# Attention with the keys on the partitions instead of transposed probabilities

## The chip, the cores and the metric

The kernel runs on one core of one Trainium2 chip. A core has a matrix engine (TensorE, in the profile PE, with its weight loads shown apart as PEld), a vector engine (DVE), a scalar engine (ACT), a general engine (POOL), DMA queues, a working memory of 128 partitions (SBUF) and an accumulator memory of eight banks (PSUM). A matmul loads a *stationary* operand (the weights, at most 128 x 128) and streams a *moving* operand of up to 512 columns past it; both have the contracted index on the partitions, and the result has the stationary operand's columns on its partitions. The metric is device time in microseconds (us); less is better. The kernel before has three timed runs and one profiled one.

## The reference

One inference step of a two-layer trunk for 512 latent tokens ("sample") and 128 context tokens ("prompt"), model width 1024. Layer 0 is gated grouped-query attention, layer 1 a bidirectional gated linear recurrence; each has an adaptive modulation of its input, an output projection and a layer norm. Everything is float32. Only the attention of layer 0 matters here:

```python
def _block_attention(q, k, v):          # q: 16 heads of 64; k, v: 4 heads of 64
    ...
    s = jnp.einsum('bqkgd,bskd->bkgqs', q_blk.astype(jnp.float32), kf) * scale
    p = jax.nn.softmax(s, axis=-1)
    return jnp.einsum('bkgqs,bskd->bqkgd', p, vf).astype(q.dtype)
```

A sample query attends to 640 keys (128 cached and 512 of its own); a prompt query attends to the 128 prompt keys. The result is multiplied by SiLU of a gate (tile `gs`) before the output projection.

## The kernel before, in words

**Number format of the scores.** Queries and keys are split into a high part and a low part, each of which the PE takes in one pass (type fp32r). For a key head `c`, tile `Xs[c]` holds four query heads with their 64 high rows and 64 low rows on the two halves of the 128 partitions (which half is which depends on `c`). `kk` holds the high part of the keys twice, once in each half; `klo` holds the low part of the keys in the half of the high queries and zeros in the other half. So one product with `kk` gives (high q + low q) times high k, and one with `klo` adds high q times low k (`score_mms`, lines 923 and 924). The probabilities and the values are plain float32, which the PE takes in several passes; the profile shows each such matmul as two records with a weight load each, and a transpose as one.

**Units of work.** The 32 sample units are (key head `c` of 4) x (query head `h` of 4) x (half `qh` of the 512 queries, so 256 queries). After four of the eight sample units of each `c` comes one prompt unit. A sample unit has these parts in `sample_unit`:

- `front(i)`, for the two blocks of 128 queries: four matmuls of 320 columns make the scores with the queries on the partitions and the 640 keys along the row (L923, L924, tile `sc`, a pair of PSUM banks); DVE takes the row's maximum, negated (L1018, `nm`); ACT takes the exponential of 640 columns with that as its bias and gives the row's sum too (L1023, `p`, `su`); two steps later DVE takes the reciprocal (L1028) and POOL scales the row (L1029).
- `trans`: ten PE transposes of 128 x 128 bring the probabilities to keys on partitions (L1036, tile `pt`), and ACT or DVE copies them to SBUF (L928, `pts`).
- `pair`/`apply`, once for two heads: ten matmuls (L950, `av_mms`) with 64 columns of the values as weights and 256 probabilities moving; the two heads lie on the two halves of the output's partitions, so that the result (`pot`) is already turned as the output projection needs it. DVE multiplies it into the gate (L955, `av_out`).

**Order of the work.** `att_gen` yields after each such part. While the attention of head `c` runs, the query projection of head `c+1` (`q_gen`: L389 to L391, norm, rotary positions, split, transposes L734), the modulation of the second layer (L312) and the loads of the next weights run as side work: `weave` advances it after each yield by a number of steps from a written table, `SIDE_AT`. `side.until("q1")` and so on force the projection to be complete before the first scores that need it. The whole first half of the program, attention included, is one block in which a planner may reorder the instructions of an engine by a simulated timeline; a few are pinned to the order of the program. The first fronts are issued in the lead-in, among the last gate projections (`gps`, L380 to L382); their exponentials are held back until that is done.

**PSUM during attention.** Two pairs of banks for scores (`b2`), three single banks (`b1`: transposes, query projections, modulation) and one (`pop`) for the result: eight in all.

## Time and profile before

| what | value |
| --- | --- |
| median of three runs | 819.64 us (819.39 to 822.28) |
| profiled execution: its time / its span | 820.92 us / 819.2 us |
| PE busy, PEld busy | 792.4 us, 700.9 us |
| DVE, ACT, POOL busy | 598.3, 447.0, 215.1 us |
| granted PE clock, mean | 0.993 |
| stretch with attention on PE | from 130.7 us (first score) to 324.5 us (last product with the values) |

How to read it: the span is the time from the first to the last profiled instruction; the execution's own time lies 1.7 us above it. "Busy" of PE is the union of records whose ends are modelled, and matmuls overlap, so the rate of the PE is read from the distance between the *starts* of successive records, not from their mean length. In a timeline row such as `229.94 1.03 PE L1036 MATMUL ... x8` the first number is the start in us, the second the length of the merged piece, x8 the number of records in it.

### The profile page before, as it was taken

Reading aid. Unit: us, or ns where it says so; the run is one execution under the profiler, and the core shown is the slowest. Engines: PE = TensorE matmul, PEld = TensorE weight load, DVE = VectorE, ACT = ScalarE, POOL = GpSimd, SP = SyncE. Lnnn points to the kernel's source line nnn. Section 1 sums busy time; section 2 is a strip of 40 time slices with the busy share of each in tenths; the row PEclk is TensorE's granted clock in tenths of the full one; section 3 lists DMA queues with packets and bytes.
Section 4 is the critical chain, followed back from the end, with each engine's and each line's share of the span. In section 5 each row is a group of like instructions: output and inputs, shape, how many; then the busy total and the mean of one; then the engine's idle time right before and its main releaser. Section 6 shows DMA issues by size and latency. Waiting matters only on the chain.

```text
span 819.2 us, 19274 instructions
## 1 busy us (share of the span) xinstructions
PE 792.4 (97%) x7953; PEld 700.9 (86%) x7953; DVE 598.3 (73%) x1083; ACT 447.0 (55%) x890; POOL 215.1 (26%) x261
## 2 busy tenths in 40 slices
PE   8999999999999989999999999999999999999994
PEld 6789999878888766888899999998999999897874
DVE  4567767686678885676799787868787876788376
ACT  2252545566566786132565666757484855766242
POOL 0124001353434843011500224122240404131121
PEclk9999999999999999999999999999999999999998
DMA  9944344234130150621431342324242344232341
GB/s 327 395 158 157 104 155 134 100 110 150 52 129 28 36 197 18 240 103 50 141 104 54 100 118 76 104 69 125 64 134 72 103 102 162 70 110 74 136 153 77
DMA packets 36630, 98.12 MB, mean 120 GB/s; under 512 B 5296, under 2 KB 12480, under 8 KB 36544
## 3 DMA queue, kind: packets, MB, share of 16 engines
q1 hardware_dynamic: 25872, 78.95, 28.7%
q0 software_dynamic: 4768, 14.18, 5.8%
q10 hardware_dynamic: 5904, 3.78, 1.6%
q8 instruction: 62, 1.02, 0.5%
q14 instruction: 24, 0.20, 0.1%
HBM read 86.06 MB, written 10.83 MB: 118 GB/s over the span
## 4 chain that ended last, share of the span: by engine, by line
PE 80%; DVE 8%; DMA 4%; ACT 3%; issue 2%; POOL 2%; SPq 0%; DVEq 0%; ACTq 0%; POOLq 0%
PE vgps L1383 8%; PE vgps L1379 4%; PE outp L1213 4%; PE outp L1215 4%; PE outp L1214 4%; PE rps L1451 4%; PE pot L950 3%; PE rps L1405 3%; PE rps L1407 3%; PE rps L1406 3%; PE pt L1036 3%; PE rps L1453 3%; PE rps L1452 3%; PE acc L568 3%; PE lv L1682 2%
## 5 line engine op out<-in xcount | busy, mean ns | idle before, releaser
L1029 POOL TENSOR_SCALAR p<-p,rc 128x640 f32<-128x640 f32 x64 | 56.9, 894 | 115.5 <-DVE rc L1028 98.3
L1720 POOL COPY At<-near 32x160 f32<-32x160 f32 x32 | 15.0, 469 | 191.8 <-PE lv L1688 173.7
L1023 ACT ACTIVATE p<-sc,nm 128x640 f32<-128x640 f32 x64 | 51.1, 801 | 25.2 <-DVE nm L1018 15.5
L1018 DVE TENSOR_REDUCE nm<-sc 128x1 f32<-128x640 f32 x64 | 51.7, 816 | 12.7 <-PE sc L924 12.6
L1405 PE MATMUL rps<-h1hi,rw 128*128 128x320 f32 x176 | 55.4, 315 | 0.0
L1407 PE MATMUL rps<-h1hi,rw 128*128 128x320 f32 x176 | 54.5, 310 | 0.1
L1406 PE MATMUL rps<-h1lo,rw 128*128 128x320 f32 x176 | 54.5, 309 | 0.0
L1036 PE MATMUL pt<-small,p 128*128 128x128 f32 x320 | 49.0, 277 | 3.0 <-DVE pts L928 1.2
L1383 PE MATMUL vgps<-rw,h1hi 128*128 128x512 f32 x180 | 48.3, 392 | 0.0
L1655 ACT COPY kc<-A 128x640 f32<-128x640 f32 x47 | 37.5, 798 | 18.5 <-DVE A L1706 12.5
L1036 PEld LDWEIGHTS pt<-small,p 128*128 128x128 f32 x320 | 36.5, 140 | 12.0 <-issue 5.6
L928 ACT COPY pts<-pt 128x512 f32<-128x512 f32 x64 | 36.1, 589 | 14.8 <-PE pt L1036 14.6
L923 PE MATMUL sc<-kk,X 128*128 128x320 f32 x128 | 42.4, 340 | 1.8 <-ACT p L1023 1.6
L1726 ACT COPY At<-lv 32x160 f32<-32x160 f32 (+1 forms) x48 | 15.8, 329 | 49.6 <-PE lv L1688 49.2
L950 PE MATMUL pot<-pts,vv 128*64 128x256 f32 x320 | 38.3, 384 | 2.1 <-DVE pts L928 2.0
L380 PE MATMUL gps<-hhi,whi 128*128 128x320 f32 x128 | 40.0, 312 | 0.1
L381 PE MATMUL gps<-hlo,whi 128*128 128x320 f32 x128 | 39.6, 309 | 0.0
L382 PE MATMUL gps<-hhi,wlo 128*128 128x320 f32 x128 | 39.5, 309 | 0.0
L1383 PEld LDWEIGHTS vgps<-rw,h1hi 128*128 128x128 f32 x180 | 33.1, 188 | 6.6
L924 PE MATMUL sc<-klo,X 128*128 128x320 f32 x128 | 38.6, 310 | 0.0
L1383 PE MATMUL vgps<-wspare,h1hi 128*128 128x512 f32 x140 | 38.1, 394 | 0.0
L389 PE MATMUL qmm<-whi,hhi 128*128 128x256 f32 x120 | 35.0, 292 | 0.1
(347 smaller groups left out, 2623.2 us busy)
## 6 DMA issues: line engine op xcount, KB each, us to landing
raw<-in_rec_w_in SPq DMA_DIRECT2D x40, 512.0 KB, 3.8
raw<-in_ada_m SPq DMA_DIRECT2D x16, 512.0 KB, 8.3
raw<-in_attn_w_in SPq DMA_DIRECT2D x16, 512.0 KB, 4.6
raw<-in_ada_s SPq DMA_DIRECT2D x16, 512.0 KB, 3.7
adaraw<-in_ada_c SPq DMA_DIRECT2D x11, 512.0 KB, 5.4
raw<-in_attn_w_out SPq DMA_DIRECT2D x8, 512.0 KB, 4.1
raw<-in_rec_w_out SPq DMA_DIRECT2D x8, 512.0 KB, 3.6
raw<-in_ada_c SPq DMA_DIRECT2D x5, 512.0 KB, 4.4
```

Source lines behind the costliest of these rows:

```text
L380: nc.tensor.matmul(ps[:, :320], w.hi(k)[:, c], hhi[:, k, t], start=(k == 0), stop=False)
L381: nc.tensor.matmul(ps[:, :320], w.hi(k)[:, c], hlo[:, k, t], start=False, stop=False)
L923: nc.tensor.matmul(out, X[:, h, t0:t0 + P], kk[:, c, k0:k1], start=True, stop=False)
L950: nc.tensor.matmul(pot[j * HD:(j + 1) * HD, :CW], vv[:, slot, c * HD:(c + 1) * HD], moving[j], start=first, stop=last)
L1018: nc.vector.tensor_reduce(nm[:, 0:1], sc[:, :, :320], AX.XY, ALU.max, negate=True)
L1023: return nc.scalar.activation(halves(p[:]), sc[:, :, :320], AF.Exp, bias=nm[:, 0:1], accum_out=su[:, 0:1])
L1029: nc.gpsimd.tensor_scalar(p, p, rs[:, 0:1], 1.0, ALU.mult, ALU.mult)
L1036: nc.tensor.transpose(pt[:, i * 256 + q * P:i * 256 + (q + 1) * P], ps[q][:, (k0 + i) * P:(k0 + i + 1) * P], ident)
L1383: nc.tensor.matmul(out, h1hi[:, k, t], wvg[i][:, k % 4].rearrange("p e n -> p (e n)"), start=(k == 0), stop=(k == KT - 1))
L1405: nc.tensor.matmul(ps[:, j, :320], hi[:, k, :], h1hi[:, k, t], start=(k == 0), stop=False)
L1406: nc.tensor.matmul(ps[:, j, :320], hi[:, k, :], h1lo[:, k, t], start=False, stop=False)
L1407: nc.tensor.matmul(ps[:, j, :320], lo[:, k, :], h1hi[:, k, t], start=False, stop=(k == KT - 1))
```

## The change

The scores are made a second time with the keys on the partitions, so that the probabilities come out of the exponential already as the product with the values needs them, and nothing of them is transposed.

- `top(i)` makes the scores as before, but with the high keys alone (two matmuls of 320 columns in place of four), only to take the row's maximum `nm`.
- `row()` makes a copy `x2` of the unit's 256 queries (ACT), turns the two columns of negated maxima into a row by two float32 matmuls (weights: the column repeated 128 times; moving: the identity) and copies that row into one partition `r` of the low half of `x2` (ACT).
- In `klo` that partition, until now zero, is set to one for the 640 sample keys. So the product of `klo` with `x2` adds the low keys' part and minus the maximum at once.
- `probs(k0, m)`, for blocks of 128 keys: one matmul with `kk` and one with `klo` as weights, 256 queries moving, into a bank of a new pool `st`; ACT takes the exponential of up to 512 columns, with neither bias nor sum.
- `apply()`, now for each unit: the probabilities (128 keys x 128 queries) are the weights, and 65 columns move: the 64 values of the key head and a column of ones (`vv` has 65 columns a head), whose product is the sum of the row. Ten matmuls a unit. After the second head of a pair, DVE takes four reciprocals and scales 256 columns (`ob`); two steps later (`D_TURN`) two transposes turn them (`turn`) and `av_out` multiplies them into the gate as before.
- POOL no longer scales anything in a sample unit. The held exponentials of the lead-in are gone.
- PSUM: one pair of banks for `top` instead of two, two single banks `st`; `b1` (three) and `pop` (one) stay. `bank_any` goes round seven places.
- `weave` takes rates by key head (`SIDE_RATES`) instead of the table. A unit now yields seven times: probs, top, apply of the unit before, probs, row of the next unit, top, probs.
- The loads and stores of the values (`cache_v`, `new_v`) move pieces of 64 numbers, because a row of `vv` is no longer contiguous.

```diff
-SIDE_AT = (
-    ...
+D_TURN = 2
+SIDE_RATES = (0.66, 0.55, 0.62, 0.15)
-def weave(main, side, steps):
-    for n, _ in enumerate(main):
-        for _ in range(int(steps[n]) if n < len(steps) else 1):
+def weave(main, side, phase, rates):
+    credit = 0.0
+    for _ in main:
+        credit += rates[phase()]
+        while credit >= 1.0:
+            credit -= 1.0
             side.step()
...
+    for e in range(2):
+        nc.gpsimd.memset(klo[HD * (1 - e):HD * (1 - e) + 1, e::2, :NT].bitcast(F32), 1.0)
-    vv = kvp.tile([P, 6, CW], F32, name="vv")
+    vv = kvp.tile([P, 6, NKV, HD + 1], F32, name="vv")
+    nc.gpsimd.memset(vv[:, :, :, HD:], 1.0)
...
-        pools["b2"] = ph.st.enter_context(pool("b2", 2, space=PSUM))
+        pools["b2"] = ph.st.enter_context(pool("b2", 1, space=PSUM))
+        pools["st"] = ph.st.enter_context(pool("st", 2, space=PSUM))
...
-        def front(i):
+        def top(i):
             sc = bank2("sc")
             for n, (k0, k1) in enumerate(HALVES):
-                score_mms(sc[:, n, :320], Xs[c], c, h, (2 * qh + i) * P, k0, k1)
+                nc.tensor.matmul(sc[:, n, :320], Xs[c][:, h, q0 + i * P:q0 + (i + 1) * P], kk[:, c, k0:k1], start=True, stop=True)
             nc.vector.tensor_reduce(nm[:, 0:1], sc[:, :, :320], AX.XY, ALU.max, negate=True)
...
-        def trans(k0, m):
...
-        def pair():
...
+        def row():
+            x2 = u["x2"] = sm.tile([P, CW], F32R, tag="x2", name="x2", bufs=2)
+            nc.scalar.copy(x2, Xs[c][:, h, q0:q0 + CW].bitcast(F32))
+            ps = bank1("row")
+            for i in range(2):
+                nc.tensor.matmul(ps[:, i * P:(i + 1) * P], view(u["nm", i], 0, [[0, P]]), ident, start=True, stop=True)
+            nc.scalar.copy(x2[r:r + 1, :], ps[r:r + 1, :CW])
+        def probs(k0, m):
+            if k0 == 0:
+                u["p"] = sm.tile([P, TT, CW], F32, tag="p", name="p", bufs=4)
+            ps = pools["st"].tile([P, 512], F32, tag="st", name="st")
+            for i in range(m):
+                k, out = slice((k0 + i) * P, (k0 + i + 1) * P), ps[:, i * CW:(i + 1) * CW]
+                nc.tensor.matmul(out, kk[:, c, k], Xs[c][:, h, q0:q0 + CW], start=True, stop=False)
+                nc.tensor.matmul(out, klo[:, c, k], u["x2"], start=False, stop=True)
+            last_exp[:] = [nc.scalar.activation(u["p"][:, k0:k0 + m, :], ps[:, :m * CW].rearrange("p (a b) -> p a b", a=m),
+                                                AF.Exp).ins]
+        def apply():
+            if j == 0:
+                outs0["po"] = pop[0].tile([P, 512], F32, tag="po", name="po")
+            po = outs0["po"]
+            for i in range(2):
+                s = (2 * i + j) * (HD + 1)
+                for k in range(TT):
+                    nc.tensor.matmul(po[:, s:s + HD + 1], u["p"][:, k, i * P:(i + 1) * P], vv[:, k, c, :],
+                                     start=(k == 0), stop=(k == TT - 1))
+            if j == 0:
+                return
+            rc = tiny.tile([P, 4], F32, tag="rc", name="rc")
+            nc.vector.reciprocal(rc, view(po, HD, [[HD + 1, 4]]))
+            ob = sm.tile([P, CW], F32, tag="ob", name="ob", bufs=2)
+            nc.vector.tensor_tensor(view(ob, 0, [[HD, 4], [1, HD]]), view(po, 0, [[HD + 1, 4], [1, HD]]),
+                                    view(rc, 0, [[1, 4], [0, HD]]), ALU.mult)
+            def turn():
+                pt = bank1("ot")
+                for i in range(2):
+                    nc.tensor.transpose(pt[:, i * P:(i + 1) * P], ob[:, i * P:(i + 1) * P], ident)
+                av_out(pt, gs[:, 2 * c + h // 2, q0:q0 + CW])
+            defer(D_TURN, turn)
...
-    weave(att, side, SIDE_AT)
+    weave(att, side, lambda: front_of[0], SIDE_RATES)
```

More of the change, by code (lines that the diff above doesn't have):

```diff
@@ L949, in av_mms @@
         for j in (1, 0):
[L950 removed]
+            nc.tensor.matmul(pot[j * HD:(j + 1) * HD, :CW], vv[:, slot, c, :HD], moving[j], start=first, stop=last)
     def av_out(pot, gt):
@@ L1055, in att_gen @@
+        return (c, [lambda: top(0), lambda: top(1)], row,
+                [lambda: probs(0, 2), lambda: probs(2, 2), lambda: probs(4, 1)], apply)
     def att_gen(side):
@@ L1068, in fronts, with rows @@
             return list(fr)
+        def rows(u):
+            return [units[u][2]] if u < len(units) and units[u][2] else []
         def run(f):
@@ L1077, in att_gen @@
                 yield
+        for f in rows(0):
+            run(f)
+            yield
         pending = []
-        def flush():
-            while pending:
-                run(pending.pop(0))
-                yield
-        for u, (c, _, back, end) in enumerate(units):
+        for u, (c, _, _, back, end) in enumerate(units):
             fr = fronts(u + AHEAD)
+            ro = rows(u + 1)
             for n, b in enumerate(back):
@@ L1098, in att_gen @@
             back_of[0] = c
-            if end:
-                pending.append(end if len(back) == 2 else end())
-        yield from flush()
+            pending.append(end)
+        for f in pending:
+            run(f)
+            yield
         while later:
```

91 lines of the change are left out of this document (23 added, 68 removed).

## The prediction

> **What bounds the kernel now.** I read the page's first two parts (how full is each engine), then the windows of the attention stretch, then the timeline of PE record by record, and last the chain that ended last.
>
> ```profile
> PE 792.4 (97%) x7953; PEld 700.9 (86%) x7953; DVE 598.3 (73%) x1083; ACT 447.0 (55%) x890; POOL 215.1 (26%) x261
> PEclk9999999999999999999999999999999999999998
> PE 80%; DVE 8%; DMA 4%; ACT 3%; issue 2%; POOL 2%; SPq 0%; DVEq 0%; ACTq 0%; POOLq 0%
> ```
>
> ```profile
> core 0: us, PE busy (x) PEld busy (x) DVE busy (x) ACT busy (x) POOL busy (x), PEclk, DMA share, GB/s
> 135.00:182.00 47.00, 46.29 (x396) 38.13 (x394) 32.05 (x78) 29.59 (x68) 19.88 (x22) 1.00 0.27 87
> 182.00:229.00 47.00, 46.94 (x410) 39.45 (x408) 30.86 (x67) 28.55 (x64) 18.62 (x21) 1.00 0.31 106
> 229.00:276.00 47.00, 46.18 (x380) 40.56 (x376) 35.47 (x76) 31.32 (x70) 24.30 (x26) 1.00 0.21 69
> 276.00:325.00 49.00, 42.70 (x325) 31.78 (x321) 36.99 (x78) 35.27 (x78) 26.41 (x26) 1.00 0.29 97
> ```
>
> The reader is to see that in the stretch with attention PE stands still for 0.71 + 0.06 + 0.82 + 6.30 = 7.9 us of 190, most of it in the last quarter, where no query projection is left to fill gaps. DVE (75% in its fullest window), ACT (72%) and POOL (54%) all have room, and the clock is full. So an instruction that PE no longer issues is worth its time, one that is added costs its time, and the work that the change takes from ACT, DVE and POOL is worth at most those 7.9 us. The sum is one of PE records.
>
> **The price of a record on PE.** Busy means overlap, so I take distances between starts.
>
> ```profile
> 244.06 0.31 PE L923 MATMUL sc<-kk,X 128*128 128x320 f32 x1
> ...
> 244.50 0.31 PE L924 MATMUL sc<-klo,X 128*128 128x320 f32 x1
> ...
> 239.24 0.28 PE L389 MATMUL qmm<-whi,hhi 128*128 128x256 f32 x1
> ...
> 240.55 0.28 PE L391 MATMUL qmm<-whi,hlo 128*128 128x256 f32 x1
> ...
> 229.94 1.03 PE L1036 MATMUL pt<-small,p 128*128 128x128 f32 x8
> ...
> 248.01 2.31 PE pot L950 x20
> ```
>
> 320 columns: three steps from 244.06 to 244.50, 0.147 us. 256 columns: eleven steps in 1.31 us, 0.119 us. A transpose: (1.03 - 0.27)/7 = 0.109 us (0.27 is the length of one, L1036 below). The ten products with the values of a pair of heads (20 records; from the chain of waits): 2.31 us.
>
> What the trace before has nowhere in bulk is what `apply` consists of: full 128 x 128 weights for only 65 moving columns. There the weight load, not the stream, may set the pace. Rows with full weights and a short or shorter stream:
>
> ```profile
> 150.56 0.19 PEld L923 LDWEIGHTS pscp<-kk,X 128*128 128x128 f32 x1 [0.64 <-ACT p L1023]
> ...
> 151.34 0.19 PEld L924 LDWEIGHTS pscp<-klo,X 128*128 128x128 f32 x1
> ```
>
> ```profile
> 7.65 0.52 PEld L330 LDWEIGHTS adaps<-small,row 128*128 128x128 f32 x4 [0.32 <-DVE row L336]
> 7.65 0.61 PE L330 MATMUL adaps<-small,row 128*128 128x2 f32 x4
> ```
>
> ```profile
> 458.77 1.86 PEld L1777 LDWEIGHTS sp<-vg,kt 128*128 128x128 f32 x16
> ```
>
> ```profile
> 231.53 0.54 PE L734 MATMUL qps<-identr,qs 128*128 128x128 f32 x4
> ```
>
> The prompt scores move 128 columns and follow each other every (151.34 - 150.56)/7 = 0.111 us, though the step from 256 to 320 columns says that a column costs (0.147 - 0.119)/64 = 0.44 ns, so 128 of them 0.056. L330 is float32 and moves 2 columns: its four loads take 0.52 us, 0.19 the last alone, so 0.11 us a load. The float32 products L1777 (128 columns, two records each): (1.86 - 0.19)/15 = 0.111 us. Three rows, streams of 2 to 128 columns, one price: **a full weight load every 0.111 us is the floor of a record.** A 65-column record is fenced in by L330 below and L1777 above, both 0.111 to 0.112; I take 0.112. The farther bounds, which I keep for the range: 0.097 us, the distance of the transposes L734, (0.54 - 0.25)/3, the cheapest records with 128-column weights; and, were the load wholly hidden, two passes of 65 columns, 2 x 65 x 0.44 ns = 0.057 us.
>
> The Trainium skill, page "TensorE: Matmul & The Clock Gate", section "Back-to-back issue gap", gives for a sustained stream of loads and matmuls at 128 columns about 81 ns each. The prompt scores above are such a stream and show 111 ns, so the trace does not agree; by the page's figure, an estimate, `apply` would be 640 x 0.081 = 51.8 us and the kernel would end near 838 us.
>
> **The change part by part, PE.**
>
> ```profile
> L923 PE MATMUL sc<-kk,X 128*128 128x320 f32 x128 | 42.4, 340 | 1.8 <-ACT p L1023 1.6
> L924 PE MATMUL sc<-klo,X 128*128 128x320 f32 x128 | 38.6, 310 | 0.0
> L1036 PE MATMUL pt<-small,p 128*128 128x128 f32 x320 | 49.0, 277 | 3.0 <-DVE pts L928 1.2
> L950 PE MATMUL pot<-pts,vv 128*64 128x256 f32 x320 | 38.3, 384 | 2.1 <-DVE pts L928 2.0
> ```
>
> Removed: 128 products with `klo`, 128 x 0.147 = 18.8 us; 320 transposes, 34.9 us; the 16 pairs' products, 16 x 2.31 = 37.0 us. Together 90.7 us. The 128 products with `kk` stay, as `top`.
>
> Added: `probs`, 32 units x 10 matmuls of 256 columns, 320 x 0.119 = 38.1 us (not below 0.111 by the load, so 35.5 at least). `row`, 64 float32 matmuls of 128 columns, two records each at L1777's price: 128 x 0.112 = 14.3 us. `apply`, 32 x 10 matmuls in two records: 640 x 0.112 = 71.7 us. `turn`, 32 transposes: 3.5 us. Together 127.6 us.
>
> Net: +36.9 us on PE. The change takes away 320 transposes but pays for that with twice the records in the products with the values (each head by itself, 128 weights for 65 columns, where before two heads of 64 weights shared the array while 256 columns streamed) and with scores made one and a half times. Three of the four windows were full of PE work and the fourth had 6.3 us free, so next to nothing hides it.
>
> **The other engines.**
>
> ```profile
> L1018 DVE TENSOR_REDUCE nm<-sc 128x1 f32<-128x640 f32 x64 | 51.7, 816 | 12.7 <-PE sc L924 12.6
> L1023 ACT ACTIVATE p<-sc,nm 128x640 f32<-128x640 f32 x64 | 51.1, 801 | 25.2 <-DVE nm L1018 15.5
> L928 ACT COPY pts<-pt 128x512 f32<-128x512 f32 x64 | 36.1, 589 | 14.8 <-PE pt L1036 14.6
> L1029 POOL TENSOR_SCALAR p<-p,rc 128x640 f32<-128x640 f32 x64 | 56.9, 894 | 115.5 <-DVE rc L1028 98.3
> ```
>
> ACT had about 0.80 x 2 for exponentials (and the reading of sums) and 0.59 x 2 of copies a unit, 2.8 us and more; it now has 640 x 2 columns of exponentials in three pieces, under 2 x 0.80, and two copies, each at most 0.59: no more than before. DVE keeps both maxima (1.63 us a unit) and loses the copies `pts`; its scaling `ob` of 256 columns once a pair replaces them. POOL loses 56.9 us that nobody but the transposes waited for. All of that I cost at nothing: PE covers it, and the cover grows. The smaller pieces of `cache_v` and `new_v` move the same bytes in the lead-in some 100 us before the first `apply` wants them; new_k and the query norms stand behind `new_v` on POOL's queue, while PE is busy with gate projections; nothing, too, as are the two memsets.
>
> **Stalls.** Of the 7.9 us of idle PE I let half of the last quarter's go (3.2 us), since `probs` no longer waits for POOL's scaling. Against that stands the single pair of banks for `top`.
>
> ```profile
> 237.06 1.22 DVE L264 TENSOR_TENSOR wlo<-raw,whi 128x1024 fp32r<-128x1024 f32 x1
> ...
> 244.84 0.82 DVE L1018 TENSOR_REDUCE nm<-sc 128x1 f32<-128x640 f32 x1 [1.86 <-PE sc L924]
> ```
>
> The reduction in the second row, of the scores whose last matmul ran from 244.50 to 244.81, starts at 244.84 and lasts 0.82, so a pair of banks is free 1.16 us after its last matmul started. In written order there lie between the second `top` of a unit and the first of the next only six `probs` matmuls, 6 x 0.119, and that last matmul's own 0.147: 0.86 us. So 0.3 us a unit are missing where no side step falls in between and the planner puts nothing there: 32 x 0.3 = 9.6 us at most if DVE is free at once. Queued behind the waiting `top` on PE are the next `apply`, `probs` and `row`, and ACT's exponentials wait for those. Side steps fall after about six yields in ten for three quarters, so I take a third: +3.2 us. Below, nothing; above, 9.6 and, with DVE busy in a weight split (1.22, the first row) now and then, some 15.
>
> The end of the stretch grows:
>
> ```profile
> 322.08 2.38 PE L950 MATMUL pot<-pts,vv 128*64 128x256 f32 x20 [0.52 <-DVE pts L928]
> ...
> 324.50 0.42 DVE L955 TENSOR_TENSOR gs<-pot,gs 128x256 f32<-128x256 f32 x1 [2.48 <-PE pot L950]
> ...
> 324.98 0.19 PEld L1213 LDWEIGHTS outp<-wohi,hhi 128*128 128x128 f32 x1 [0.98 <-DVE gs L955]
> ```
>
> Between the last product and the output projection lay one DVE step of 0.42. Now a reciprocal, `ob` (another 0.42 or so) and two transposes with 0.27 of latency come before it: +1.2 us.
>
> **Sum.** +36.9 (PE records) - 3.2 (old stalls) + 3.2 (new ones) + 1.2 (end) = +38.1 us. Against the profiled execution, 820.9 us, that makes 859.0; the median of the runs lies 1.3 us below that execution, so 857.7, say **858 us**.
>
> **The rivals.**
>
> *Faster: the 65 columns cost their stream.* If the load of the next weights hid fully behind the stream, `apply` would take 640 x 0.057 = 36.5 us, 35.2 less, and net PE work would grow by 1.7 us only; the freed engines could then give back most of the 7.9 us of idle time. 820.9 + 1.7 - 7 = 815.6, on the scale of the median 814. For it: loads do run beside matmuls (PEld is a row of its own). Against it: L330, with 2 columns, still takes 0.11 us a record. It decides as soon as a 65-column record falls under about 0.06 us. Chance 0.06.
>
> *Partly hidden: 0.097 us a record*, as L734 shows for transposes: 640 x 0.015 = 9.6 us less, 848. Against it: transposes' loads are recorded shorter (L734's kind 0.14, as for L1036, the others 0.19). Chance 0.12. The 81 ns of the Trainium skill's page, cited above, would lie past this case, at 838; I give it no chance of its own.
>
> *The new waits decide.* The single pair of banks, and the chain maximum, row, copy on ACT, `klo` product, hold PE up in each unit, and the rates of the side work leave stretches without filler: +10 to 15 us above my forecast, some 870. For it: the last quarter before had 6.3 us of gaps with two pairs of banks. Against it: in the same block the planner moved records even within a score, and the longer PE time a unit gives DVE and ACT more room. Chance 0.22.
>
> **How the numbers follow.** The forecast itself, PE records at the load's price and stalls about as before (850 to 864), has 0.57; 0.03 is left for no change at all by something I don't see. The range runs from 843 (5 us below the partly hidden case) to 876 (the waits, with a few us on top); outside it I leave about 0.06 + 0.06 below and 0.05 above. A measurement of this kernel tells about 0.5%, 4 us, from no change. Faster by more: 0.07; within: 0.03; slower: 0.90.
>
> **What would show it.** Right: in the changed profile the records of `apply` (some 640, 128*128 weights, 65 columns) follow each other at 0.11 us and PE is full from 135 us to about 360; POOL is nearly empty there; the stretch after the output projection keeps its length and only starts later. Wrong: `apply` records closer than 0.1 us; the same number of them in pairs that overlap; or gaps on PE before `top` that name `nm`, above 5 us in total. What would make me wrong as a whole is a price of a short record that none of L330, L1777 and the prompt scores has.

## The result, and the profile after

The changed kernel takes **864.17 us** (861.82 to 867.22, four runs) against 819.51 us (819.26 to 822.28, four runs) for the kernel before on the same chip: a ratio of **1.054, 95% interval 1.050 to 1.058**. The forecast was 858, between 843 and 876. The profiled execution of the changed kernel took 864.14 us with a span of 862.4, so the two spans differ by 43.2 us where the prediction's sum said 38.1.

The page's first parts, for the changed kernel (busy time of each engine, the granted clock in 40 slices):

```profile
PE 833.4 (97%) x8305; PEld 758.9 (88%) x8305; DVE 589.8 (68%) x1019; ACT 428.7 (50%) x858; POOL 160.9 (19%) x200
PEclk9999899999999999999999999999999999999997
```

PE has 41.0 us more of busy time and 352 records more; DVE, ACT and POOL have all got less. There is one digit below 9 early in the clock's row (the fifth slice, 86 to 108 us), which before had not; the last digit of both kernels is the end of the span.

**Where the 43.2 us lie.** Three marks cut the span: the last gate projection (`gps`, L382), which ends the lead-in, and the first output projection (`outp`), which ends the attention. Timeline rows of PE, before and then after:

```profile
134.06 0.31 PE L382 MATMUL gps<-hhi,wlo 128*128 128x320 f32 x1
```

```profile
139.27 0.31 PE L382 MATMUL gps<-hhi,wlo 128*128 128x320 f32 x1
...
367.48 0.50 PE L1214 MATMUL outp<-wohi,hhi 128*128 128x512 f32 x1 [0.52 <-DVE gs L961]
```

Before, the output projection began at 324.98. So the lead-in got 139.27 - 134.06 = **5.2 us longer**; the attention went from 324.98 - 134.06 = 190.9 to 367.48 - 139.27 = 228.2, **37.3 us longer**; and what follows went from 819.2 - 324.98 = 494.2 to 862.4 - 367.48 = 494.9, **0.7 us longer**.

**The attention.** Windows of the changed kernel over this stretch (columns as in the prediction: length, then busy time and records of PE, PEld, DVE, ACT, POOL, then clock, DMA share, GB/s):

```profile
139.30:196.00 56.70, 56.55 (x502) 52.61 (x502) 32.93 (x65) 26.54 (x60) 7.44 (x8) 1.00 0.31 104
196.00:253.00 57.00, 55.51 (x489) 50.83 (x488) 31.31 (x56) 25.30 (x61) 7.46 (x8) 1.00 0.25 86
253.00:310.00 57.00, 55.34 (x457) 53.01 (x456) 36.45 (x65) 26.42 (x62) 12.94 (x9) 1.00 0.14 45
310.00:367.50 57.50, 52.86 (x421) 49.10 (x420) 27.93 (x50) 28.50 (x66) 3.78 (x4) 1.00 0.19 65
```

PE is idle for 228.2 - 220.26 = 7.9 us, as long as before, at full clock. The stretch is longer by PE's records alone. POOL is busy for a seventh of it, DVE and ACT for about half.

Timeline rows of PE in the middle of it, with runs of the new records:

```profile
199.74 1.39 PE L1041 MATMUL po<-vv,p 128*128 128x65 f32 x11
...
202.21 0.28 PE L1029 MATMUL st<-X,kk 128*128 128x256 f32 x1
202.33 0.28 PE L1030 MATMUL st<-x,klo 128*128 128x256 f32 x1
...
204.39 0.61 PE L1020 MATMUL row<-small,nm 128*128 128x128 f32 x4
```

From start to start: `apply` (1.39 - 0.27)/10 = **0.112 us** a record, with 0.27 the length of one; `probs` 0.12; `row` (0.61 - 0.27)/3 = 0.113. These are the three prices that the prediction had put in from other rows.

**The lead-in.** The page of the changed kernel has one long wait there. Timeline rows of PE, and the window behind the wait:

```profile
85.97 1.25 PE L739 MATMUL qps<-identr,qs 128*128 128x128 f32 x8 [3.62 <-DVE qs L731]
...
89.28 0.47 PE L382 MATMUL gps<-hhi,wlo 128*128 128x320 f32 x1
89.55 0.47 PE L380 MATMUL gps<-hhi,whi 128*128 128x320 f32 x1
```

```profile
85.00:91.50 6.50, 5.53 (x25) 5.54 (x26) 4.07 (x7) 2.92 (x5) 0.00 (x0) 0.50 0.00 1
```

The transposes of the first queries (`qps`) stand on PE before gate projections that are ready, and wait 3.6 us for DVE. Then the clock is at half: the gate records follow each other at 0.27 us (89.28 to 89.55) where 0.147 is their pace, from 84.7 to 91.6 us. The wait itself takes the first 1.2 of these 6.8 us; in the other 5.6 half is lost. 3.6 + 2.8 = 6.4 us, of which 5.2 remain at the end of the lead-in.

### The profile page after: what moved, and what is told of

Read it like the earlier page. It is cut to its first block, busy times and chain, and to the rows that moved or that the text cites. A ratio compares the mean times of both kernels' runs of the same rounds, so it can differ in the third digit from the quotient of the medians.

```text
span 862.4 us, 19652 instructions
## 1 busy us (share of the span) xinstructions
PE 833.4 (97%) x8305; PEld 758.9 (88%) x8305; DVE 589.8 (68%) x1019; ACT 428.7 (50%) x858; POOL 160.9 (19%) x200
## 3 DMA queue, kind: packets, MB, share of 16 engines
q8 instruction: 65, 1.06, 0.5%
## 4 chain that ended last, share of the span: by engine, by line
PE 81%; DVE 10%; DMA 3%; ACT 3%; issue 2%; POOL 1%; SPq 0%; DVEq 0%; ACTq 0%; POOLq 0%
PE vgps L1384 7%; PE po L1041 7%; PE vgps L1380 4%; PE outp L1214 4%; PE outp L1216 4%; PE outp L1215 4%; PE rps L1452 3%; PE acc L570 3%; PE rps L1454 3%; PE rps L1453 3%; PE rps L1406 2%; PE rps L1408 2%; PE rps L1407 2%; PE lv L1683 2%; PE st L1029 2%; PE gps L380 2%
## 5 line engine op out<-in xcount | busy, mean ns | idle before, releaser
L1031 ACT ACTIVATE p<-st 128x512 f32<-128x512 f32 (+1 forms) x96 | 47.9, 525 | 67.0 <-PE st L1030 66.4
L1041 PE MATMUL po<-vv,p 128*128 128x65 f32 x640 | 79.8, 271 | 0.9 <-ACT p L1031 0.9
L1041 PEld LDWEIGHTS po<-vv,p 128*128 128x128 f32 x640 | 77.3, 192 | 2.5 <-ACT p L1031 1.3
L1029 PE MATMUL st<-X,kk 128*128 128x256 f32 x160 | 48.6, 317 | 1.8 <-ACT p L1031 1.4
L213 POOL TENSOR_TENSOR rstd<-rs_t,mhalf 128x8 f32<-128x8 f32 (+1 forms) x9 | 12.9, 1432 | 167.2 <-DVE rs_t L212 167.1
L1030 PE MATMUL st<-x,klo 128*128 128x256 f32 x160 | 42.0, 294 | 1.0 <-ACT x L1021 0.9
L382 PE MATMUL gps<-hhi,wlo 128*128 128x320 f32 x128 | 40.4, 315 | 0.0
L1384 PEld LDWEIGHTS vgps<-rw,h1hi 128*128 128x128 f32 x180 | 33.1, 188 | 6.9 <-DVE rw L264 0.4
L1029 PEld LDWEIGHTS st<-X,kk 128*128 128x128 f32 x160 | 30.1, 190 | 4.6 <-ACT p L1031 3.6
L390 PE MATMUL qmm<-wlo,hhi 128*128 128x256 f32 x120 | 34.0, 284 | 0.0
```

Of the source, the lines that this page charges most:

```text
L382: nc.tensor.matmul(ps[:, :320], w.lo(k)[:, c], hhi[:, k, t], start=False, stop=(k == KT - 1))
L1029: nc.tensor.matmul(out, kk[:, c, k], Xs[c][:, h, q0:q0 + CW], start=True, stop=False)
L1030: nc.tensor.matmul(out, klo[:, c, k], u["x2"], start=False, stop=True)
L1031: last_exp[:] = [nc.scalar.activation(u["p"][:, k0:k0 + m, :], ps[:, :m * CW].rearrange("p (a b) -> p a b", a=m), AF.Exp).ins]
L1041: nc.tensor.matmul(po[:, s:s + HD + 1], u["p"][:, k, i * P:(i + 1) * P], vv[:, k, c, :], start=(k == 0), stop=(k == TT - 1))
L1384: nc.tensor.matmul(out, h1hi[:, k, t], wvg[i][:, k % 4].rearrange("p e n -> p (e n)"), start=(k == 0), stop=(k == KT - 1))
```

## The experiments

Theory 1, the prediction's own: PE is full in the attention, and a record of `apply` costs its weight load, 0.112 us, whatever it moves; the part of the miss that lies in the lead-in comes from `bank_any`. The rivals were that the moved columns set the price, and that waits do. The runs of the kernel before beside these runs had medians of 819.8 to 821.8 us, so a difference of 2 us or less between the medians of two experiments tells nothing by itself. The edits are made on the changed kernel; 864.2 us is what they are held against. Their attention is measured from the end of the last gate projection to the first output projection; by that measure the changed kernel has 367.48 - 139.58 = 227.9 us and the kernel before 324.98 - 134.37 = 190.6.

**1. Twice the columns in `apply`** (values read past their end into the next head's; the surplus columns are read by nobody):

```diff
-                s = (2 * i + j) * (HD + 1)
+                s = (2 * i + j) * P
-                    nc.tensor.matmul(po[:, s:s + HD + 1], u["p"][:, k, i * P:(i + 1) * P], vv[:, k, c, :],
+                    nc.tensor.matmul(po[:, s:s + P], u["p"][:, k, i * P:(i + 1) * P], view(vv, (k * NKV + c) * (HD + 1), [[1, P]]),
```

> As the changed kernel, but each product with the values moves 128 columns instead of 65 (the 65 and what stands behind them in the tile; the further columns are not used). Theory 1, a record with 128 x 128 weights costs its weight load, 0.112 us, and its columns nothing up to about 128: no change, 862 to 867 us, and the 640 records of apply still follow each other at 0.111 to 0.112 us. Rival, the columns set the price: 640 records x 63 columns x 2 passes x 0.44 ns = 35 us more, about 900 us.

Measured: 862.8 us (862.2 to 863.6), ratio 1.052 (1.048 to 1.055). From its timeline:

```profile
190.36 1.95 PE L1041 MATMUL po<-vv,p 128*128 128x128 f32 x16
```

(1.95 - 0.27)/15 = 0.112 us. Nearly twice the columns cost nothing, so the 65 columns do not set the price; that the load does is shown by a row of experiment 4. The prediction's rival "the 65 columns cost their stream" has fallen. The Trainium skill, page "TensorE: Matmul & The Clock Gate", section "LDWEIGHTS (loading the stationary operand)", has a load cost its columns divided by 1.2, in ns; for 128 columns that makes 107 ns, an estimate. The 112 ns here agree within 5%.

**2. `bank_any` round six places, in the order before:**

```diff
-        n = spin[0] % 7
+        n = spin[0] % 6
...
-        if n < 3:
+        if n == 1:
...
-        return pop[0].tile(...) if n == 3 else bank1(name)[:]
+        return pop[0].tile(...) if n == 2 else bank1(name)[:]
```

> As the changed kernel, but the lead-in goes round six PSUM places in the order of the kernel before instead of seven. The planner then puts 117 gate matmuls ahead of the first turned queries instead of 72 (96 before). Theory: the 3.6 us for which PE waited at 82 to 86 us in the changed kernel, and the 6.8 us at half clock right behind it, come from that order: they go, the last gate matmul ends near 134 us instead of 139, and the kernel takes 858 to 860 us. Rival: the clock falls there for a reason that has nothing to do with the order, and the wait is found elsewhere: 864 us.

Measured: 860.5 us (860.0 to 862.2), ratio 1.050 (1.046 to 1.053). Its windows over the lead-in, and the last gate projection:

```profile
82.00:85.00 3.00, 3.00 (x22) 3.00 (x22) 2.31 (x4) 0.44 (x1) 0.58 (x1) 1.00 0.00 0
85.00:91.50 6.50, 5.97 (x44) 5.65 (x42) 4.33 (x7) 2.22 (x5) 0.00 (x0) 1.00 0.00 0
```

```profile
134.79 0.31 PE L382 MATMUL gps<-hhi,wlo 128*128 128x320 f32 x1
```

The long wait and the half clock are gone, and the lead-in ends 139.27 - 134.79 = 4.5 us sooner. Nothing else was touched, so the extra time in the lead-in came with the seven places: with another rotation of banks the planner puts the transposes of the first queries elsewhere among the gate projections. How much time that costs depends on the order that it finds: over all the runs, the lead-in ends between 132.7 and 137.2 us with six places and between 137.1 and 140.5 with seven, and the same kernel traced twice (experiment 8) gave 133.1 and 134.9. Of the 4.5 us, 3.7 arrive in the medians; the attention is 1.9 us longer here (135.10 to 364.92), 1.0 of it idle PE (8.9 us, experiment 4) and the rest left open.

**3. The row of maxima in one fp32r pass with one weight column** (64 records in place of 128, and nearly no load; the maxima are rounded to fp32r):

```diff
-            nm = u["nm", i] = tiny.tile([P, 4], F32, tag="nm", name="nm", bufs=8)
+            nm = u["nm", i] = tiny.tile([P, 4], F32R, tag="nm", name="nm", bufs=8)
-                nc.tensor.matmul(ps[:, i * P:(i + 1) * P], view(u["nm", i], 0, [[0, P]]), ident, start=True, stop=True)
-            nc.scalar.copy(x2[r:r + 1, :], ps[r:r + 1, :CW])
+                nc.tensor.matmul(ps[:1, i * P:(i + 1) * P], view(u["nm", i], 0, [[0, 1]]), identr, start=True, stop=True)
+            nc.scalar.copy(x2[r:r + 1, :], ps[0:1, :CW])
```

> As the changed kernel, but the row of negated maxima is made with one column of weights and in one pass (fp32r, the maximum rounded to it; the sum uses the same rounded maximum) instead of 128 equal columns of float32 in two records. Theory 1, PE records set the time: 128 records of 0.112 us become 64 of 0.056 (their stream) to 0.111: 7 to 11 us less, 853 to 857 us. Rival, the row costs by its chain (maxima, row, copy by ACT, klo product) and not by its records: 862 to 865 us.

Measured: 866.4 us (863.4 to 871.0), ratio 1.057 (1.052 to 1.061): **a miss**, no gain. Its timeline at 320 to 323 us (of the execution of 871.0 us, the longest of the four), and a window behind that:

```profile
319.97 1.04 ACT L262 CAST wohi<-raw 128x1024 fp32r<-128x1024 f32 x1 [3.69 <-DMA raw<-in_attn_w_out]
...
321.05 1.23 DVE L264 TENSOR_TENSOR wolo<-raw,wohi 128x1024 fp32r<-128x1024 f32 x1 [4.14 <-ACT wohi L262]
322.19 0.82 DVE L1013 TENSOR_REDUCE nm<-sc 128x1 fp32r<-128x640 f32 x1
323.06 0.90 PE L1011 MATMUL sc<-kk,X 128*128 128x320 f32 x2 [3.78 <-DVE nm L1013]
```

```profile
325.00:340.00 15.00, 15.00 (x71) 14.58 (x70) 3.41 (x6) 4.19 (x10) 1.53 (x1) 0.50 0.00 1
```

Read from the top: a weight's transfer lands late, ACT waits for it and DVE for ACT; behind DVE's weight split stands the reduction of the maxima, and PE waits for the one pair of banks of `top`, 3.8 us. Then the clock is at half for at least 15 us, half of which is lost. Over the whole attention (140.3 to 374.2 us) PE is idle for 11.8 us against 7.9, and 0.05 of clock over 234.0 us are about 11.7: together more than the 10.5 us that the records were to give. That is the prediction's third rival (the single pair of banks, with DVE in a weight split) happening once, and made dear by the clock.

**4. Edits 2 and 3 together.**

> Change: the first two of these edits without the third: six places, and the row in one fp32r pass with one weight column. Theory 1 (e3_row saved its PE time, but one stall of 4 us behind a late weight transfer and the half clock after it took that back): 860.5 - 10.5 = 850 us, 847 to 853. Rival (the row's records are hidden beside other work or their time comes back as waits, so the saving never shows): 859 to 866, as in e3_row.

Measured: 857.6 us (855.8 to 858.8), ratio 1.043 (1.039 to 1.047): 2.9 us better than experiment 2 (4.9 by the distance of each to the kernel before beside it), where 10.5 were expected; a miss again, in the direction of theory 1. The window over the whole attention, this run and then experiment 2:

```profile
132.70:361.40 228.70, 218.39 (x1795) 199.46 (x1794) 127.04 (x235) 105.61 (x248) 31.62 (x29) 0.98 0.23 75
```

```profile
135.10:364.90 229.80, 220.95 (x1858) 205.52 (x1857) 128.18 (x235) 106.61 (x248) 31.60 (x29) 1.00 0.22 74
```

The attention is 1.1 us shorter, and the lead-in ends 2.4 us sooner. Idle PE went from 8.9 to 10.3 us, and 0.02 of clock over 228.7 us are about 4.6 us: some 6 us of the saving went there, and with the 1.1 the records gave about 7 of the 10.5.

The run also shows what a record costs whose load is small. In the timeline row below two records of `row`, 128 columns moving past weights of one column, stand together:

```profile
212.68 0.28 PE L1020 MATMUL row<-identr,nm 128*1 128x128 f32 x2
```

With 0.22 the length of one, they follow each other at 0.28 - 0.22 = 0.06 us, where the prompt scores of the prediction, with as many columns moving in the same format but 128 columns of weights, take 0.111. So the load is what a full record costs. (Not every record of `row` is so cheap: the median distance to the next record is 0.06, for a quarter of them it is 0.14.)

**5. The values as weights again**, as before the change, two heads side by side on the array and 256 probabilities moving; the sums of a row from additions on POOL and a product with ones, and the reciprocal of 128 x 256 of them on DVE:

```diff
-                    nc.tensor.matmul(po[:, s:s + HD + 1], u["p"][:, k, i * P:(i + 1) * P], vv[:, k, c, :], ...)
...
+            nc.gpsimd.tensor_tensor(h2, p[:, 0:2, :], p[:, 2:4, :], ALU.add)
+            nc.gpsimd.tensor_tensor(t, h2[:, 0, :], h2[:, 1, :], ALU.add)
+            nc.gpsimd.tensor_tensor(t, t, p[:, 4, :], ALU.add)
...
+            for k in range(TT):
+                av_mms(pot, k, c, [w["p"][:, k, :] for w in both], k == 0, k == TT - 1)
...
+                    nc.tensor.matmul(pot[i * HD:(i + 1) * HD, CW:], view(vv, HD, [[0, HD]]), both[i]["t"], start=True, stop=True)
+                nc.vector.reciprocal(ob, pot[:, CW:])
```

> As the changed kernel, but the product with the values is turned back: the values (64 columns) are the weights, 256 probabilities move, two heads side by side, as before the change. The sums are made by POOL adding the five key blocks of a unit and one matmul a head with ones as weights; no reciprocal on four columns, no turning transposes. Theory 1: apply and turn, 640 x 0.112 + 3.5 = 75 us, become 16 x (2.31 + 0.43) = 44 us; 31 us less, 831 to 836 us. Rival 1, the added time was mostly in new waits (single pair of score banks, row chain): these stay, so 845 us or more. Rival 2, POOL's adding (some 2.8 us a unit) comes late and holds up the next: 840 to 850 us, with PE waiting for tile t.

Measured: 879.5 us (877.8 to 880.2), ratio 1.072 (1.069 to 1.075): **a miss by over 40 us**. Groups of its attention, and the window over it:

```profile
L1038 POOL TENSOR_TENSOR h<-p 128x512 f32<-128x512 f32 x32 | 44.0, 1374 | 132.9 <-ACT p L1031 111.9 <-PE st L1030 21.0
...
L1059 DVE RECIPROCAL ob<-po 128x256 f32<-128x256 f32 x16 | 28.1, 1755 | 14.6 <-PE po L1057 14.6
...
L264 DVE TENSOR_TENSOR wlo<-raw,whi 128x1024 fp32r<-128x1024 f32 x5 | 7.4, 1473 | 0.9 <-ACT whi L262 0.9
```

```profile
139.60:381.50 241.90, 217.02 (x1570) 164.53 (x1569) 167.50 (x236) 106.56 (x248) 131.47 (x125) 0.95 0.21 71
```

The reciprocal takes 1.76 us where the four columns of the changed kernel take 0.18, and some of DVE's other operations are slower in this run, in which POOL is busy for 131 us of the stretch (the weight split takes 1.47 us, against 1.22 in the kernel before; that POOL is the cause is not shown). PE stands for 24.9 us, 17.0 more than in the changed kernel, and 0.05 of clock over 241.9 us are another 12. For POOL's sums PE waits only 0.6 us, so the second rival did not happen; it waits most for ACT's copies into `x2` and its exponentials (6.0 and 4.6 us). Some 16 us of the miss are left, and most of them lie in PE's rows: each time PE goes from 128 columns of weights to 64 and back, some 0.24 us pass beside the price of the records (median). That happens 52 times here, 13 us in all, because the products are cut into short runs; before the change it happened 21 times, 4.7 us. So this run does not separate PE's terms; it shows that this version as a whole costs more than it frees.

**6. The product in one pass** (probabilities written as fp32r by the exponential, a copy `vr` of the values in fp32r with 66 columns a head; both are rounded to that format):

```diff
+    vr = kvp.tile([P, TT, NKV, HD + 2], F32R, name="vr")
-                u["p"] = sm.tile([P, TT, CW], F32, tag="p", name="p", bufs=4)
+                u["p"] = sm.tile([P, TT, CW], F32R, tag="p", name="p", bufs=4)
-                    nc.tensor.matmul(po[:, s:s + HD + 1], u["p"][:, k, i * P:(i + 1) * P], vv[:, k, c, :],
+                    nc.tensor.matmul(po[:, s:s + HD + 2], u["p"][:, k, i * P:(i + 1) * P], vr[:, k, c, :],
```

> Change: the product of the probabilities with the values goes in one pass: the probabilities are written as fp32r by the exponential, and a copy of the values (with two columns of ones) is kept in fp32r, so both are rounded to that format. 320 records with a full weight load in place of 640; nothing else of the attention changes. Theory 1 (PE is full, and a record costs its weight load, 0.112 us): 864.2 - 320 x 0.112 = 828 us, 825 to 833. Rival A (from here on the chain maximum, row, copy, low product and the single pair of banks sets the time, so that PE empties and only half of it comes back): about 846. Rival B (something outside PE sets the length of the attention): no change, 860 to 866.

Measured: 844.5 us (841.5 to 846.1), ratio 1.027 (1.023 to 1.031). The window over its attention:

```profile
140.50:346.20 205.70, 191.64 (x1539) 174.35 (x1537) 128.09 (x236) 106.47 (x248) 31.82 (x29) 0.98 0.24 83
```

The attention is 227.9 - 205.7 = 22.2 us shorter, where 35.8 were taken away. Idle PE rose from 7.9 to 14.1 us, and 0.02 of clock over 205.7 us are about 4.1 us. 22.2 + 6.2 + 4.1 = 32.5: the records cost what theory 1 says, within some 3 us, but a third of it came back as waits and as clock. In time alone the run lies at rival A.

**7. No maximum** (`top` and `row` left out, the exponential of an eighth of the score):

```diff
-            sc = bank2("sc")
-            ...
+            pass
-                nc.tensor.matmul(out, klo[:, c, k], u["x2"], start=False, stop=True)
+                nc.tensor.matmul(out, klo[:, c, k], Xs[c][:, h, q0:q0 + CW], start=False, stop=True)
```

> Change: the maximum is left out of the sample units: no scores with queries on partitions (128 matmuls of 320 columns), no reduction, no row, no copy of the queries; the low product takes the queries themselves. The exponential is taken of an eighth of the score, so that nothing overflows. What is left is scores with keys on partitions, exponential, product and turn, the least that this way of doing it costs. Theory 1: PE sheds 128 x 0.147 + 128 x 0.112 = 33.1 us, and DVE and the single pair of banks are out of the way, so up to 3 us of stalls go too: 828 to 832 us, still above the kernel before. Rival (waits on the maxima, not records, are what the attention has gained over before): they all go with it, 815 or less.

Measured: 826.7 us (825.3 to 830.7, eight runs), ratio 1.007 (1.005 to 1.010).

```profile
137.10:329.50 192.40, 184.22 (x1605) 171.84 (x1604) 80.29 (x171) 84.73 (x184) 32.78 (x29) 1.00 0.27 89
```

This version is no longer the softmax of the reference; it only prices what is left out. The attention sheds 227.9 - 192.4 = 35.5 us for 33.1 us of records; the other 2 us of the median lie in the lead-in, which ends 2.5 us sooner. PE's idle time did not shrink (192.40 - 184.22 = 8.2 us, 7.9 in the changed kernel), so the waits behind the maxima cost next to nothing on balance, and 0.147 and 0.112 were the right prices for these 256 records within 2.4 us. The second reading is the more telling one: with no maximum at all the attention is still as long as the whole attention before (190.6). By the prediction's prices `probs`, `apply` and `turn` alone (113.3 us) eat up what both score products, the transposes and the pair products had cost (109.5 us).

**8. Edits 2, 3 and 6 together**, and the same kernel once more, beside the run of experiment 10:

> Change: three edits together on the changed kernel: the single PSUM banks go round six places in the order before (as in e2_six), the row of maxima is turned in one fp32r pass with one weight column (as in e3_row), the product with the values goes in one pass (as in e6_onepass; probabilities and values rounded to fp32r). Theory 1: 860.5 (measured for the first edit) - 10.5 (row: 128 x 0.112 = 14.3 to 64 x 0.06 = 3.8) - 35.8 (320 x 0.112) = 814 us, 811 to 822: level with the kernel before or a little faster. Rival A (the chain behind the maxima and the single pair of banks bind as soon as PE has room; gaps of 3 to 4 us then halve the clock for a while): 830 to 840.

> The kernel of e8_six_one_row once more, unchanged, on the chip of the run beside it. Theory S: 833 to 837 us and a half clock for some 30 us of the attention again, since the gaps follow from the order of the instructions. Rival C (the clock of e8_six_one_row was a matter of that chip): 825 to 830, clock as in e11_one_wide.

Measured: 835.3 us (833.4 to 837.0), ratio 1.016 (1.013 to 1.020), and again 834.6 us (833.7 to 838.7), ratio 1.018 (1.014 to 1.022). Where theory 1 had 814, 20 us are missing. The windows over the attention and, in the first of the two runs, around two places where the clock falls:

```profile
133.10:338.30 205.20, 192.53 (x1474) 172.81 (x1473) 127.10 (x236) 105.47 (x248) 32.20 (x29) 0.92 0.25 83
```

```profile
229.73:233.14 3.41, 2.30 (x19) 1.90 (x17) 2.83 (x4) 3.15 (x8) 0.00 (x0) 1.00 0.56 182
233.14:243.38 10.24, 9.06 (x39) 8.24 (x39) 4.97 (x10) 1.78 (x5) 0.00 (x0) 0.50 0.25 90
291.17:294.58 3.41, 2.25 (x20) 1.97 (x18) 3.38 (x6) 2.04 (x5) 0.00 (x0) 1.00 0.74 293
294.58:315.06 20.48, 19.98 (x89) 18.61 (x89) 9.10 (x14) 9.32 (x21) 1.70 (x1) 0.50 0.33 123
```

0.08 of clock over 205.2 us are 16.4 us, and idle PE has 12.7 us against 8.9 in experiment 2. These two make up the missing 20. The clock falls here without a long wait: the longest one on PE between 285 and 316 us is 1.3 us. In the 3.4 us ahead of the fall PE was busy for two thirds.

**9. Edit 8 with 128 columns in each record of `apply`**, and with `turn` a step later as well (`D_TURN = 3`):

```diff
-                    nc.tensor.matmul(po[:, s:s + HD + 2], u["p"][:, k, i * P:(i + 1) * P], vr[:, k, c, :],
+                    nc.tensor.matmul(po[:, s:s + P], u["p"][:, k, i * P:(i + 1) * P], vrt[:, (k * NKV + c) * (HD + 2):(k * NKV + c) * (HD + 2) + P],
```

> Change: as e8_six_one_row (835.2 us there, clock 0.92 in the attention, 16 us lost to it, no gap on PE above 1.3 us), but each record of the product with the values moves 128 columns instead of 66; the added columns are read by nobody. Their price should stay 0.112 us, the weight load, as e1_wide showed for the float32 form. Theory S (the clock is granted by how many columns PE streams in a stretch of 3.4 us, and records that stream 66 columns in the time of 128 count as idle): the added columns cost nothing and bring the clock back; 820 to 828 us, clock in the attention 0.97 or more. Rival I (only the gaps between records count): 832 to 838, clock as in e8_six_one_row. Rival P (a one-pass record of 128 columns costs more than one of 66): above 840.

> Change: as e11_one_wide, and the two transposes that turn the scaled result come three steps after the product instead of two (in e8_six_one_row PE waited 2.1 us for the scaled tile). If waits of PE are what is left: 2 us less than e11_one_wide. Rival (the later turn holds its bank or the last steps longer): the same or 1 us more.

Measured: 829.1 us (823.9 to 831.0), ratio 1.009 (1.006 to 1.012), clock over the whole span 0.980 to 0.990 in six executions, against 0.969 to 0.977 in the eight executions of experiment 8. With the later turn: 829.5 us (825.6 to 831.6), ratio 1.009 (1.006 to 1.012), so the later turn does nothing that shows.

```profile
136.70:331.60 194.90, 182.24 (x1474) 162.61 (x1472) 127.41 (x236) 105.39 (x248) 32.09 (x29) 0.98 0.26 87
```

```profile
203.62 1.23 PE L1048 MATMUL po<-vr,p 128*128 128x128 f32 x10
```

A kernel in which PE moves nearly twice as many columns, the surplus read by nobody, is 6 us *faster*, and the two intervals do not meet: the ten records above take (1.23 - 0.27)/9 = 0.107 us each, PE idles as long as in experiment 8 (12.7 us), and the clock in the attention went from 0.92 to 0.98. The attention is 10.3 us shorter; the lead-in of this run ends 3.6 us later. One doubt stays: with the wider records the planner also put the instructions in another order. The last section comes back to it.

**10. Edit 6 with 128 columns**, to see the same on another order:

> Change: as e6_onepass (844.5 us, clock 0.92 in the last fifth of the attention, 4 us lost to the clock there and some 3 us more around 85 us), but each record of the product with the values moves 128 columns instead of 66, as e11_one_wide did to e8_six_one_row. Theory S (columns streamed in a stretch of 3.4 us decide on the clock): up to 4 us less, 839 to 843, and no half clock inside the attention. Rival O (e11_one_wide gained because the planner ordered the records otherwise): 842 to 849, with half clock in the attention as before.

Measured: 843.1 us (840.0 to 845.7), ratio 1.027 (1.024 to 1.030), clock 0.985 to 0.991 in four executions against 0.977 to 0.985. The clock moves the same way, but half clock inside the attention is still there (0.99 over the stretch), against the expectation, and the 1.4 us in time are less than these runs can tell.

None of the versions beats the kernel before; the nearest that computes the whole function lies 0.9% above it, and only with rounded probabilities and values.

## Why the prediction was right, and what it missed

The number and the sign were right, and the mechanism is the one that was forecast: PE was full, it still is, and the attention is longer by its records.

- **`apply`, 640 x 0.112 us:** right. The record's distance is 0.112, and with 128 columns it is the same (experiment 1). The partly hidden case (0.097) did not come. The Trainium skill, page "TensorE: Matmul & The Clock Gate", section "Back-to-back issue gap", has about 81 ns for a sustained stream of loads and matmuls at 128 columns. The 112 ns here do not agree, as the prediction expected from the prompt scores' row.
- **`top` halved, `row`, `probs`, `turn`:** right. Taking `top` and `row` out gave 35.5 us in the attention for 33.1 of records, with idle PE unchanged (experiment 7).
- **Net +36.9 us on PE, +38.1 with stalls and end:** the attention, for which this sum was made, grew by 37.3 us, PE's busy time in it by 220.0 - 182.7 = 37.3.
- **Stalls, -3.2 and +3.2:** about right in their sum, idle PE being 7.9 us in both kernels (with the end's +1.2 it was to be 9.1); wrong in their place, so the sum was luck in part. The waits of PE in the changed kernel's attention, by what they wait for (total, times, longest):

```profile
PE ot L1054 <- DVE ob L1048: 2.5, 6, 0.7
PE st L1029 <- ACT p L1031: 1.4, 3, 0.9
PE sc L1011 <- DVE nm L1013: 0.9, 2, 0.6
```

The wait for the single pair of banks (`nm`), which the prediction priced at 3.2 us, is 0.9 us; the largest is for the scaled tile ahead of the transposes of `turn`, which the sum had only at the very end of the stretch.
- **The end, +1.2 us:** right. From the last product to the output projection before 324.98 - 324.46 = 0.5; after 367.48 - 365.79 = 1.7 (last product 364.73 + 1.06, below).

```profile
364.73 1.06 PE L1041 MATMUL po<-vv,p 128*128 128x65 f32 x8
...
365.82 0.18 DVE L1046 RECIPROCAL rc<-po 128x4 f32<-128x4 f32 x1 [6.22 <-PE po L1041]
366.04 0.42 DVE L1048 TENSOR_TENSOR ob<-po,rc 128x256 f32<-128x256 f32 x1
366.52 0.44 PE L1054 MATMUL ot<-small,ob 128*128 128x128 f32 x2 [0.73 <-DVE ob L1048]
```

- **What failed: the lead-in.** The sum has no term for `bank_any`, though the diff shows its seven places, and what it says of the lead-in (transfers, memsets) ends in "nothing". It cost 5.2 of the 6.4 us between the sum (857.7) and the median; of the rest, 0.7 lie behind the attention, -0.8 in it, and 1.3 come from the step from execution to median, which this time was nothing (864.14 and 864.17). Experiment 2 gave 4.5 of the 5.2 us back. The mechanism was not priced because the edit adds no instruction. In a block that a planner orders, a change of the banks' rotation changes the order, and there one wait of 3.6 us and the half clock behind it were the outcome.
- **The rival "the new waits decide":** it did not come in the changed kernel, but it is near. Experiment 3 met it once, and as soon as PE got room (6 and 8) idle PE rose by 4 to 6 us.

## What to carry to other kernels

A matmul that turns the probabilities into weights pays a full weight load for 65 columns of use, so removing the transposes is worth their time only where the product does not get more records in exchange: count records times the price of a load first, columns second. An edit that adds no instruction but changes a rotation of buffers ahead of a planner needs a term of its own: here a wait of 3.6 us with 5.6 us of half clock behind it. On a full PE, count a saving twice: what it takes from the records, and what the thinner stream then loses to waits and to the clock.

## What the runs showed of the hardware that was not expected

**The clock falls when PE streams too few columns, even without a long pause.** In every trace here the granted clock changes in steps of 3.4 us and is either full or half. The wait of 3.6 us in the lead-in brought half clock, from 2.4 us after its start. The Trainium skill, page "TensorE: Matmul & The Clock Gate", section "What's actually happening", gives an idle window of about 3.4 us as the cause of that. The trace agrees only in part: the last 3.4 us at full clock (81.3 to 84.7 us) were not idle throughout, PE was busy for 1.0 us of them. And experiment 8 lost the clock after windows with PE busy for 2.25 and 2.30 of 3.41 us and no wait above 1.3 us, once for 20 us. Busy time alone does not decide either: the kernel before kept full clock after a window with less.

```profile
279.00:282.41 3.41, 1.89 (x17) 1.19 (x18) 3.41 (x8) 2.70 (x6) 3.41 (x3) 1.00 0.28 64
```

What decides can be read from the records. Cut each trace into the clock's own steps of 3.41 us and add up how long PE streams columns in each: 0.417 ns a column, from the lengths of records of 512 and 320 columns, (0.389 - 0.309)/192 us; a float32 record counts twice, since with 256 columns it lasts 0.379 us where one of fp32r lasts 0.283; the streaming is laid at the end of the record. In the 14 traces, between 25 and 810 us, there are 32 steps at full clock with half clock behind them, and they stream at most 1.33 us. The 3109 that kept full clock stream at least 1.24 us, and only 5 of them less than 1.33. By PE's busy time the two kinds are not apart: up to 2.72 us ahead of a fall, down to 1.78 us without one, with 74 of the steps that kept full clock below 2.72.

The two steps of experiment 8 stream 1.26 and 1.15 us, the one of the kernel before 2.88. So a record that streams 66 columns in the time of a whole load counts by its columns and not by its time. With 128 columns counted in place of 66, in the same order of instructions, the two steps of experiment 8 would have 1.51 and 1.36 us, above the limit: the columns are enough to explain experiment 9, without the order. This is a count over the traces, not an experiment of its own; experiment 9 did change the order as well, and 10 moved the clock by less than could be told in time. The Trainium skill's same page, section "A second HAM failure mode: psum-queue depth-cycling", tells of short idle times between groups of matmuls that let the clock swing. That is nearer to experiment 8 than the idle window, but no run here tests it alone.

**The clock halves the load's pace too.** At half clock a record of `apply` takes about twice its 0.112 us, so the price of a load goes with PE's clock. Two timeline rows of experiment 8 at half clock, of two records and of eight: the six records between them cost (1.75 - 0.47)/6 = 0.213 us each.

```profile
295.29 0.47 PE L1046 MATMUL po<-vr,p 128*128 128x66 f32 x2
295.93 1.75 PE L1046 MATMUL po<-vr,p 128*128 128x66 f32 x8
```

**A reciprocal is dear by its columns.** On DVE 1.755 us for 256 columns (experiment 5), 0.18 for 4 (the row at 365.82): (1.755 - 0.18)/252 = 6.3 ns a column. The scaling of 256 columns (`ob`, the row at 366.04) takes 0.42 us. The sixteen reciprocals of experiment 5 lie between 1.744 and 1.759 us, although other operations of DVE were slower in that run.
